# A hybrid decoder block on one core: the MLP's up projection with weights prepared four products ahead and its squares summed one per product, the down projection's buffers laid out anew

## The chip, the cores and the metric

The kernel runs on one core of a Trainium2 chip. The metric is the device time of one execution in microseconds (us). The engines named below are PE (TensorE, the matrix products; PEld is its loading of weights), DVE (VectorE), ACT (ScalarE), POOL (GpSimd) and SP (SyncE, which here issues nearly all transfers between HBM and the on-chip memory SBUF; SPq is its queue). Products are summed up in PSUM banks, which DVE and ACT read.

## The reference

One layer, on 2048 rows of 1024 columns, all float32. The part that the change touches is the last one:

```python
h = h + jnp.concatenate([y_s5, y_rwkv], axis=-1) @ w_out          # the output projection
hn = rms_norm(h, norm_ffn_g)
h = h + jnp.square(jax.nn.relu(hn @ w_up)) @ w_down               # 1024 -> 4096 -> 1024
return rms_norm(h, norm_final_g)
```

What comes ahead (a norm, an input projection, an S5 state-space mixer, an RWKV-7 mixer) is left as it is.

## The kernel before

**Products.** A float32 operand is split into a high half (`hi`, a cast to the type that PE takes, by ACT) and a low half (`lo = x - hi`, by DVE); a product of two operands is three products of halves, hi·hi, hi·lo and lo·hi. Above that the kernel multiplies 2x2 blocks by seven products in place of eight (Strassen's scheme in Winograd's form). The seven are numbered 1 to 7 and are written in the order `ORDER = (1, 5, 6, 2, 7, 3, 4)`; the sums of blocks that they need are made on POOL (`left_sums`, for the up weights: four sums in each set of seven) or on DVE or POOL (`right_sums`). Three PSUM tiles take the seven: `ps_ua` takes 1, then 6, 7 and 4 on top, and is read after each; `ps_ux` takes 5, then 3; `ps_ub` takes 2.

**Up projection, `mlp_up`.** Two halves of the rows (`hb`, 1024 rows each), and in each 16 steps of `f`: 32 blocks in all, here called block 0 to block 31. A block has seven products of 12 matmuls (128x128 by 128x512), 84 in all. The left operand is the weights: `ws()` loads them (`wraw`, seven buffers `raw`, which other loads share), makes the sums, and splits each into `wh` (ACT, L1423) and `wl` (DVE, L1424), in a ring of 16 buffers with the tag `ys`. `Ahead(ws(), UA)` runs that generator `UA` products ahead of the one that is written. The right operand is the normed activations `x1` to `x7`, split by `xs(hb)` once for each half of the rows: at the start, with the sums on DVE, and for the second half during block 15, with the sums on POOL. Blocks 1 and 2 also carry the last two pieces of the norm (`last_norm`: loads `hrow`, transposes `ps_tr`).

After product 2, 7, 3 and 4 one quarter of the block's result is complete: it gets relu and square (`finish`, ACT L1499 and L1500), as `q[1]`, `q[4]`, `q[3]` and `q[2]`. The down projection needs the sums of these quarters as its left operands: `operands` writes three of them plain to HBM (`hr_d`) and makes four sums, split into halves `hh` and `hl` in the same ring `ys` and written to HBM (`hs_d`). Before, three of the four sums come right after product 3, the fourth after product 4.

**Down projection, `mlp_down`.** Eight groups `gr` of the 4096 inner columns, and in each eight chunks `c` of 256 rows; a chunk has seven products of six matmuls. Weights `w_down` are loaded into `wraw` (two buffers of 1 MB), summed and split into `w0` to `w8`; the hidden operands are loaded back, the plain ones (`hr`) and split here, the summed ones (`hs`) as they are. The sums run in 16 tiles `acc` of 512 KB, which are loaded from `h_d` first. Product 1 of chunk 0 needs `w0` and the first `hr`.

**Order.** A scheduler orders the instructions of each engine; each engine then runs its own list strictly in that order, and waits on semaphores where one needs another's result. SP's list is one queue of issues. Pools of the down projection lie where pools of the up projection lay, and a tile can be filled only when the last use of the tiles under it is over. So the places of the pools in `mlp_down` decide how early its loads can be issued.

Of the kernel before, what the change touches and what calls it, by code (L numbers as in the profile page):

```python
# [7 lines left out]
F32 = mybir.dt.float32  # L8
# [3 lines left out]
ALU = mybir.AluOpType  # L12
# [3 lines left out]
P = 128  # L16
# [6 lines left out]
def pool_of(tc, **k):  # L23
    return tc.tile_pool(reuse_waits="tile", **k)
# [339 lines left out]
BT = 512  # L364
# [709 lines left out]
        yield  # L1074


UA, DW, DH = 2, 2, 3
WS, WA = 9, 3
OB = 256

# [241 lines left out]
def product(K, ps, left, right, start):  # L1322

    (lh, ll), (rh, rl) = left, right
    n = len(lh)
    for k in range(n):
        for i, (a, b) in enumerate(((lh, rh), (lh, rl), (ll, rh))):
            K.nc.tensor.matmul(ps, a[k], b[k], start=start and k + i == 0, stop=k == n - 1 and i == 2, skip_group_check=True)  # L1328
# [27 lines left out]
PLAIN = (1, 2, 4)  # L1356


def mlp_up(K, opened, h_dram, x2_dram, norm_g, w_up, hs_dram, hr_dram):


    nc, tc = K.nc, K.tc
    v, act, g = nc.vector, nc.scalar, nc.gpsimd
    H = KT // 2
    from contextlib import ExitStack
    with ExitStack() as st:
        pool_ = lambda **k: st.enter_context(pool_of(tc, **k))
        oc, oy, ops, last = opened
        xp, rp, cp, hp, psp = pool_(name="mux", bufs=1), pool_(name="mur", bufs=1), pool_(name="muc", bufs=1), pool_(name="muh", bufs=1), pool_(name="mups", bufs=2, space=PSUM)
# [57 lines left out]
        def last_norm(b):  # L1427

            ss, rows, junk = cp.tile([P, 2], F32, tag="ss", name="ss"), [raw([P, 1024], "hrow") for _ in range(2)], raw([P, 1024], "junk")
            for i, r in enumerate(rows):  # L1430
                nc.sync.dma_start(out=r, in_=h_dram[(2 * b + i) * P:(2 * b + i + 1) * P, :])
                act.activation(out=junk, in_=r, func=AF.Square, accum_out=ss[:, i:i + 1])
            rs = rms_rows(K, cp, ss, 2, 1024, "rstd")
            for i, r in enumerate(rows):
                v.tensor_scalar(out=r, in0=r, scalar1=rs[:, i:i + 1], scalar2=None, op0=ALU.mult)
            yield
            for k in range(KT):
                if k % 4 == 0:
                    o = raw([P, 4, 256], "xt")
                if k % 2 == 0:  # L1440
                    ps = ops.tile([P, BT], F32, tag="t2", bufs=1, name="ps_tr")
                    for i in range(4):
                        nc.tensor.transpose(out=ps[:, i * P:(i + 1) * P], in_=rows[i % 2][:, (k + i // 2) * P:(k + i // 2 + 1) * P], identity=K.ident)
                act.activation(out=o[:, k % 4], in_=ps[:, k % 2 * 256:k % 2 * 256 + 256], func=AF.Copy, scale=gain[:, k:k + 1])
                if k % 4 == 3:
                    nc.sync.dma_start(out=x2_dram[b // 2, :, k - 3:k + 1, b % 2 * 256:b % 2 * 256 + 256], in_=o)
                if k % 2:
                    yield
# [10 lines left out]
        def hid(name):  # L1459
            nonlocal ct  # L1460
            ct = (ct + 1) % 6
            return hp.tile([P, BT], F32, tag="o", bufs=3, name=name) if ct < 3 else oc[0].tile([P, BT], F32, tag=("g2h", "g2l", "g2s")[ct - 3], name=name)

        def operands(hb, fp, q, done):

            def plain(n):
                nc.sync.dma_start(out=hr_dram[hb, fp, PLAIN.index(n)], in_=q[n])

            def split_(n, o):
                hi, lo = (oy.tile([P, BT], F32R, tag="ys", bufs=16, name="h" + s) for s in "hl")  # L1470
                act.copy(out=hi, in_=o)  # L1471
                v.tensor_tensor(out=lo, in0=o, in1=hi.bitcast(F32), op=ALU.subtract)
                for i, t in enumerate((hi, lo)):
                    nc.sync.dma_start(out=hs_dram[hb, SPLIT.index(n), fp, i], in_=t.bitcast(F32))

            if done in (1, 4):
                plain(done)
            elif done == 3:
                a, c, d = q[1], q[3], q[4]
                s = hp.tile([P, BT], F32, tag="s", bufs=2, name="hs")  # L1480
                v.tensor_tensor(out=s, in0=c, in1=d, op=ALU.add)
                split_(5, s)
                v.tensor_tensor(out=c, in0=a, in1=c, op=ALU.subtract)
                split_(7, c)
                q["s2"] = s2 = hp.tile([P, BT], F32, tag="s", bufs=2, name="hs2")
                v.tensor_tensor(out=s2, in0=s, in1=a, op=ALU.subtract)
                split_(6, s2)
            else:
                plain(2)
                s = hp.tile([P, BT], F32, tag="s", bufs=2, name="hs3")  # L1490
                v.tensor_tensor(out=s, in0=q[2], in1=q["s2"], op=ALU.subtract)  # L1491
                split_(3, s)

        for hb in range(2):
            for f in range(0, 32, 2):
                q = {}

                def finish(o, name, src=None):
                    act.activation(out=o, in_=o if src is None else src, func=AF.Relu)  # L1499
                    act.activation(out=o, in_=o, func=AF.Square)  # L1500
                    q[name] = o
                    operands(hb, f // 2, q, name)

                def copy(ps, name):
                    o = hid(name)
                    act.copy(out=o, in_=ps)
                    return o

                A, X = (psp.tile([P, BT], F32, tag=n, bufs=2, name="ps_u" + n) for n in "ax")
                B = ops.tile([P, BT], F32, tag="o", bufs=2, name="ps_ub")  # L1510
                for n in ORDER:
                    lw = w.take()
                    if n not in x:
                        next(nx)
                    ps, start = {1: (A, True), 5: (X, True), 6: (A, False), 2: (B, True), 7: (A, False), 3: (X, False), 4: (A, False)}[n]
                    product(K, ps, lw, x[n], start)
                    if f in (2, 4) and hb == 0:
                        if n == 1:
                            ln = last_norm(NT // 256 - 3 + f // 2)
                        next(ln, None)  # L1520
                    if f == 30 and hb == 0:
                        if n == 1:
                            nx = xs(1)
                        next(nx)
                    if n == 1:
                        c1 = copy(A, "c1")
                    elif n == 5:
                        c5 = copy(X, "c5")
                    elif n == 6:
                        c2 = copy(A, "c2")  # L1530
                    elif n == 2:
                        v.tensor_tensor(out=c1, in0=c1, in1=B, op=ALU.add)  # L1532
                        finish(c1, 1)
                    elif n == 7:
                        v.tensor_tensor(out=c5, in0=c5, in1=A, op=ALU.add)
                        finish(c5, 4)
                    elif n == 3:
                        v.tensor_tensor(out=c2, in0=c2, in1=X, op=ALU.add)
                        finish(c2, 3)
                    else:  # L1540
                        finish(hid("c4"), 2, A)


def mlp_down(K, h_dram, hs_dram, hr_dram, w_down, fin_g, out):

    nc, tc = K.nc, K.tc
    v, act, g = nc.vector, nc.scalar, nc.gpsimd
    NG, NC = 8, NT // 256
    from contextlib import ExitStack
    with ExitStack() as st:  # L1550
        pool_ = lambda **k: st.enter_context(pool_of(tc, **k))

        hp, fp, wp1, rp, ap2 = (pool_(name="md" + n, bufs=1) for n in ("h", "f", "w1", "r", "a2"))
        wp2, wp3, ap1 = (pool_(name="md" + n, bufs=1, side="right") for n in ("w2", "w3", "a1"))
        psp = pool_(name="mdps", bufs=2, space=PSUM)
        wpool, apool = [wp1] * 6 + [wp2] + [wp3] * 2, [rp] * 2 + [ap1] * 8 + [ap2] * 2 + [wp3] * 4
        rows = lambda c: [(c // 4) * 1024 + i * BT + c % 4 * P for i in range(2)]

        def ws():
# [95 lines left out]
def hybrid_block(tc, a, cst, out):  # L1655
# [3 lines left out]
    with ExitStack() as st:  # L1659
# [44 lines left out]
        with ExitStack() as keep:  # L1704
            opened = out_proj(K, keep, a["x"], g_d, y_d, f_d, s_d, *A("g2", "ln_x_w", "ln_x_b", "w_glu", "b_glu", "s5_out_g", "w_out", "norm_ffn_g"), h_d, x2_d)
            mlp_up(K, opened, h_d, x2_d, a["norm_ffn_g"], a["w_up"], hs_d, hr_d)
        mlp_down(K, h_d, hs_d, hr_d, a["w_down"], a["norm_final_g"], out)


# [16 lines left out]
```

## Time and profile before

| | |
|---|---|
| median of 3 runs | 2716.64 us (2715.95 to 2719.07) |
| the profiled execution: its own time | 2711.46 us |
| its span, first to last instruction | 2709.7 us |
| mean granted PE clock | 0.965 of full speed |
| up projection, first matmul | 1266.5 us into the span |
| down projection, first matmul | 2029.1 us into the span |

A window row gives the length of a stretch, the busy time of each engine in it with the number of its instructions (x), the granted PE clock, the mean busy share of the 16 DMA engines and the GB/s that they moved. A group row gives an operation's count, its busy time and mean duration, and then the idle time of its engine just ahead of it with what ended it. A wait row gives who waited for whom: total, times, longest. A timeline row gives a start, a duration and the instruction.

### The profile page before, as it was taken

How to read it: one execution, taken by the hardware profiler on the slowest of the kernel's cores; microseconds unless marked ns; L12 is line 12 of the kernel's file. 1: busy time of each engine (PE TensorE's matmuls, PEld its weight loads, DVE VectorE, ACT ScalarE, POOL GpSimd, SP SyncE). 2: the span in 40 equal slices, each digit the busy share in tenths (PEclk: the TensorE clock that was granted, in tenths of full speed). 3: DMA queues.
4: the chain of work that ended last, by engine and by line, in shares of the span. 5: the costliest groups of instructions: out<-in, count | busy, mean ns of one | idle time of the engine just before them, and what ended most of it. 6: DMA issues, size and time to landing. Idle time of an engine off the chain costs nothing.

```text
span 2709.7 us, 38217 instructions
## 1 busy us (share of the span) xinstructions
PE 2486.5 (92%) x13084; PEld 2027.1 (75%) x13084; DVE 1910.2 (70%) x3177; ACT 1307.2 (48%) x2558; POOL 926.5 (34%) x812
## 2 busy tenths in 40 slices
PE   7999889998998989997899987999969999999997
PEld 7977667786998878886777765777747777777775
DVE  7478896688777777667677778776756666555665
ACT  5355545554544465553656555555543333332333
POOL 1068788502222233212322235322212323232333
PEclk9999989998999999999999998999989999999999
DMA  9556648996866464334655544555467555455545
GB/s 297 190 173 178 207 140 254 253 221 175 174 152 155 108 195 150 136 134 156 209 195 191 192 176 167 180 186 179 162 230 264 181 170 163 148 167 171 167 145 181
DMA packets 543187, 492.55 MB, mean 182 GB/s; under 512 B 187312, under 2 KB 445360, under 8 KB 542992
## 3 DMA queue, kind: packets, MB, share of 16 engines
q1 hardware_dynamic: 542704, 489.05, 58.0%
q8 instruction: 104, 1.70, 0.3%
q10 hardware_dynamic: 288, 1.05, 0.1%
q14 instruction: 91, 0.75, 0.1%
HBM read 304.27 MB, written 180.49 MB: 179 GB/s over the span
## 4 chain that ended last, share of the span: by engine, by line
PE 59%; DVE 16%; DMA 10%; issue 6%; ACT 5%; POOL 3%; SPq 1%; POOLq 0%; DVEq 0%; ACTq 0%
PE ps_ua L1328 12%; PE ps_da L1328 9%; PE ps_dx L1328 4%; PE ps_ux L1328 3%; PE ps_ub L1328 3%; PE ps_db L1328 2%; DMA wraw<-in_w_down 2%; PE ps_o L435 2%; PE ps_o L433 2%; PE ps_o L434 2%; DVE hs L1491 2%; PE ps_z L433 1%; PE ps_z L434 1%; PE ps_z L435 1%; PE ps_b L817 1%
## 5 line engine op out<-in xcount | busy, mean ns | idle before, releaser
L1605 POOL TENSOR_TENSOR acc<-acc,c 128x512 f32<-128x512 f32 x128 | 193.8, 1535 | 482.0 <-ACT c L1609 436.4
L1609 ACT COPY c<-ps_da 128x512 f32<-128x512 f32 x192 | 106.2, 588 | 266.0 <-PE ps_da L1328 265.5
L433 PE MATMUL ps_z<-xh,wh 128*128 128x512 f32 x448 | 184.9, 413 | 16.0 <-DVE zr L617 6.4
L435 PE MATMUL ps_z<-xh,wl 128*128 128x512 f32 x448 | 182.3, 407 | 0.0
L434 PE MATMUL ps_z<-xl,wh 128*128 128x512 f32 x448 | 181.4, 405 | 0.0
L1605 DVE TENSOR_TENSOR acc<-acc,ps_dx 128x512 f32<-128x512 f32 x128 | 87.6, 685 | 126.6 <-PE ps_dx L1328 121.4
L1424 DVE TENSOR_TENSOR wl<-wraw,wh 128x512 fp32r<-128x512 f32 x128 | 163.2, 1301 | 4.6 <-ACT wh L1423 1.8
L1300 POOL TENSOR_TENSOR ws<-wraw,ws 128x512 f32<-128x512 f32 x32 | 43.5, 1360 | 347.7 <-DVE wl L1424 342.1
L1499 ACT ACTIVATE c<-c 128x512 f32<-128x512 f32 x96 | 60.6, 631 | 165.8 <-DVE c L1532 101.5
L374 ACT CAST hh<-hr 128x512 fp32r<-128x512 f32 x96 | 59.6, 621 | 125.6 <-PE ps_da L1328 88.6
L433 PEld LDWEIGHTS ps_z<-xh,wh 128*128 128x128 f32 x448 | 87.7, 196 | 40.7 <-DVE zr L617 8.2
L609 DVE TENSOR_TENSOR wl<-wr,wh 128x1024 fp32r<-128x1024 f32 x56 | 85.2, 1522 | 36.4 <-ACT wh L608 34.3
L913 POOL TENSOR_TENSOR DT<-dtc,cst 128x128 f32<-128x128 f32 x128 | 56.0, 467 | 157.1 <-PE ps_pq L920 104.7
L433 PE MATMUL ps_o<-woh,ys 128*128 128x512 f32 x256 | 102.6, 401 | 1.5 <-ACT ys L1114 0.9
L434 PEld LDWEIGHTS ps_z<-xl,wh 128*128 128x128 f32 x448 | 87.7, 196 | 18.9 <-issue 0.9
L435 PEld LDWEIGHTS ps_z<-xh,wl 128*128 128x128 f32 x448 | 87.4, 195 | 19.2 <-issue 0.5
L434 PE MATMUL ps_o<-wol,ys 128*128 128x512 f32 x256 | 101.6, 398 | 0.0
L435 PE MATMUL ps_o<-woh,ys 128*128 128x512 f32 x256 | 100.7, 397 | 0.0
L1424 DVE TENSOR_TENSOR wl<-ws,wh 128x512 fp32r<-128x512 f32 x96 | 92.9, 968 | 1.7 <-ACT wh L1423 1.7
L1471 ACT CAST hh<-hs 128x512 fp32r<-128x512 f32 x96 | 59.8, 623 | 58.2 <-DVE hs L1491 49.7
L377 DVE TENSOR_TENSOR hl<-hr,hh 128x512 fp32r<-128x512 f32 x96 | 67.9, 712 | 26.1 <-ACT hh L374 25.9
L1500 ACT ACTIVATE c<-c 128x512 f32<-128x512 f32 x128 | 81.0, 633 | 3.5
(692 smaller groups left out, 8287.4 us busy)
## 6 DMA issues: line engine op xcount, KB each, us to landing
hs<-hs_d SPq DMA_DIRECT2D x128, 512.0 KB
wraw<-in_w_up SPq DMA_DIRECT2D x64, 512.0 KB
hs_d<-hh SPq DMA_DIRECT2D x128, 256.0 KB
hs_d<-hl SPq DMA_DIRECT2D x128, 256.0 KB
wr<-in_w_in SPq DMA_DIRECT2D x56, 512.0 KB
hr_d<-c SPq DMA_DIRECT2D x96, 256.0 KB
hr<-hr_d SPq DMA_DIRECT2D x96, 256.0 KB
xrow<-in_x SPq DMA_DIRECT2D x32, 512.0 KB
```

Of the source, the lines that this page charges most:

```text
L377: (lo_eng or nc.vector).tensor_tensor(out=lo, in0=raw, in1=hi.bitcast(F32), op=ALU.subtract)
L433: K.nc.tensor.matmul(out, lh, rh, start=i == 0, stop=False)
L434: K.nc.tensor.matmul(out, lh, rl, start=False, stop=False)
L435: K.nc.tensor.matmul(out, ll, rh, start=False, stop=i == n - 1)
L609: v.tensor_tensor(out=wl, in0=wr, in1=wh.bitcast(F32), op=ALU.subtract)
L1328: K.nc.tensor.matmul(ps, a[k], b[k], start=start and k + i == 0, stop=k == n - 1 and i == 2, skip_group_check=True)
L1424: v.tensor_tensor(out=lo, in0=o, in1=hi.bitcast(F32), op=ALU.subtract)
L1471: act.copy(out=hi, in_=o)
L1499: act.activation(out=o, in_=o if src is None else src, func=AF.Relu)
L1500: act.activation(out=o, in_=o, func=AF.Square)
L1605: add = lambda eng, o, s: eng.tensor_tensor(out=o, in0=o, in1=s, op=ALU.add)
L1609: act.copy(out=t, in_=ps)
```

## The change

Three edits. `UA` goes from 2 to 4. `operands` becomes a generator that makes one of the four sums at each step; it is advanced after product 4 of its own block and after products 1, 5 and 6 of the next (`pend`), and the plain quarters are written right where they are finished. The pools of `mlp_down` get other places: the pool of `wraw` and the first two `acc` tiles (`rp`) moves down on the left side, below the weights' pool, and the `acc` tiles and the later weights change sides.

```diff
-UA, DW, DH = 2, 2, 3
+UA, DW, DH = 4, 2, 3
@@ mlp_up
-        def operands(hb, fp, q, done):
-
-            def plain(n):
-                nc.sync.dma_start(out=hr_dram[hb, fp, PLAIN.index(n)], in_=q[n])
+        def operands(hb, fp, q):
...
-            if done in (1, 4):
-                plain(done)
-            elif done == 3:
-                a, c, d = q[1], q[3], q[4]
-                s = hp.tile([P, BT], F32, tag="s", bufs=2, name="hs")
-                v.tensor_tensor(out=s, in0=c, in1=d, op=ALU.add)
-                split_(5, s)
-                v.tensor_tensor(out=c, in0=a, in1=c, op=ALU.subtract)
-                split_(7, c)
-                q["s2"] = s2 = hp.tile([P, BT], F32, tag="s", bufs=2, name="hs2")
-                v.tensor_tensor(out=s2, in0=s, in1=a, op=ALU.subtract)
-                split_(6, s2)
-            else:
-                plain(2)
-                s = hp.tile([P, BT], F32, tag="s", bufs=2, name="hs3")
-                v.tensor_tensor(out=s, in0=q[2], in1=q["s2"], op=ALU.subtract)
-                split_(3, s)
-
+            a, c, d = q[1], q[3], q[4]
+            s = hp.tile([P, BT], F32, tag="s", bufs=2, name="hs")
+            v.tensor_tensor(out=s, in0=c, in1=d, op=ALU.add)
+            split_(5, s)
+            yield
+            v.tensor_tensor(out=c, in0=a, in1=c, op=ALU.subtract)
+            split_(7, c)
+            yield
+            v.tensor_tensor(out=s, in0=s, in1=a, op=ALU.subtract)
+            split_(6, s)
+            yield
+            s3 = hp.tile([P, BT], F32, tag="s", bufs=2, name="hs3")
+            v.tensor_tensor(out=s3, in0=q[2], in1=s, op=ALU.subtract)
+            split_(3, s3)
+
+        pend = iter(())
...
-                    operands(hb, f // 2, q, name)
+                    if name in PLAIN:
+                        nc.sync.dma_start(out=hr_dram[hb, f // 2, PLAIN.index(name)], in_=o)
...
                         finish(hid("c4"), 2, A)
+                        pend = operands(hb, f // 2, q)
+                    if n in (4, 1, 5, 6):
+                        next(pend, None)
+        for _ in pend:
+            pass
@@ mlp_down
-        hp, fp, wp1, rp, ap2 = (pool_(name="md" + n, bufs=1) for n in ("h", "f", "w1", "r", "a2"))
-        wp2, wp3, ap1 = (pool_(name="md" + n, bufs=1, side="right") for n in ("w2", "w3", "a1"))
+        hp, fp, rp, wp1, ap2 = (pool_(name="md" + n, bufs=1) for n in ("h", "f", "r", "w1", "a2"))
+        ap1, wp2 = (pool_(name="md" + n, bufs=1, side="right") for n in ("a1", "w2"))
...
-        wpool, apool = [wp1] * 6 + [wp2] + [wp3] * 2, [rp] * 2 + [ap1] * 8 + [ap2] * 2 + [wp3] * 4
+        wpool, apool = [wp1] * 4 + [wp2] * 5, [rp] * 2 + [ap1] * 10 + [ap2] * 4
```

The lists of the engines are the same up to the start of the up projection, and PE's is the same again after the down projection's first chunks. Three places show what moves in between. The changed kernel's line numbers differ by a few: L1535 becomes L1531, L1481 L1475, L1472 L1469, L1491 L1485.

DVE in a block of the steady part, before: from `c += ps_ua` (product 7 complete) on, the four sums of the squares with their low halves, and only then the weights.

```order
L1535 TENSOR_TENSOR c_17623<-c_17623,ps_ua 128x512
L1481 TENSOR_TENSOR hs<-c_17642,c_17623 128x512
L1483 TENSOR_TENSOR c_17642<-c_17605,c_17642 128x512
L1486 TENSOR_TENSOR hs_17724<-hs,c_17605 128x512
L1472 TENSOR_TENSOR hl<-hs,hh 128x512
L1472 TENSOR_TENSOR hl<-c_17642,hh 128x512
L1472 TENSOR_TENSOR hl<-hs_17724,hh 128x512
L1424 TENSOR_TENSOR wl<-ws,wh 128x512
L1491 TENSOR_TENSOR hs_17754<-c_17750,hs_17724 128x512
L1472 TENSOR_TENSOR hl<-hs_17754,hh 128x512
L1424 TENSOR_TENSOR wl<-ws,wh 128x512
L1424 TENSOR_TENSOR wl<-wraw,wh 128x512 x2
```

The same place now:

```order
L1531 TENSOR_TENSOR c_17599<-c_17599,ps_ua 128x512
L1475 TENSOR_TENSOR hs<-c_17624,c_17599 128x512
L1478 TENSOR_TENSOR c_17624<-c_17572,c_17624 128x512
L1469 TENSOR_TENSOR hl<-hs,hh 128x512
L1424 TENSOR_TENSOR wl<-wraw,wh 128x512
L1481 TENSOR_TENSOR hs<-hs,c_17572 128x512
L1469 TENSOR_TENSOR hl<-c_17624,hh 128x512
L1424 TENSOR_TENSOR wl<-ws,wh 128x512
L1469 TENSOR_TENSOR hl<-hs,hh 128x512
L1424 TENSOR_TENSOR wl<-wraw,wh 128x512
L1528 TENSOR_TENSOR c_17749<-c_17749,ps_ub 128x512
L1485 TENSOR_TENSOR hs_17803<-c_17717,hs 128x512
```

The weights' low halves now stand between the sums, one after each. Counted through the lists: where `c += ps_ua` stands, the `wl` ahead of it reach two products past the matmuls that it waits for before, and some four to seven now; at `c += ps_ub` they reach four before, two to six now. Where the second half's activations are split, the reach falls to 0.2 in block 15 and 0.4 in block 16 now, and is two to four before.

SP where the up projection ends, before. `c_19690` is the last quarter of block 31, finished after the last matmul of the up projection; `hr` and `hs` are the down projection's first operands, `wraw` its first weights.

```order
L1467 DMA hr_d<-c_19690 128x512
L1474 DMA hs_d<-hh 128x512
L1474 DMA hs_d<-hl 128x512
L1580 DMA hs<-hs_d 128x4x256 x2
L1584 DMA hr<-hr_d 128x2x256 x2
L1580 DMA hs<-hs_d 128x4x256
L1584 DMA hr<-hr_d 128x2x256
L1565 DMA wraw<-in_w_down 128x2x1024 x2
L1601 DMA acc_19772<-h_d 128x1024
```

The same place now; `c_19636` is the last quarter here, `c_19515` and `c_19542` those after products 2 and 7 of block 31.

```order
L1566 DMA wraw<-in_w_down 128x2x1024 x2
L1471 DMA hs_d<-hh 128x512
L1471 DMA hs_d<-hl 128x512
L1602 DMA acc_19737<-h_d 128x1024
L1602 DMA acc_19739<-h_d 128x1024
L1636 DMA fin<-in_norm_final_g 128x1024
L1498 DMA hr_d<-c_19515 128x512
L1498 DMA hr_d<-c_19542 128x512
L1498 DMA hr_d<-c_19636 128x512
L1471 DMA hs_d<-hh 128x512
L1471 DMA hs_d<-hl 128x512
L1471 DMA hs_d<-hh 128x512
```

The weights' loads have moved from behind the last quarter and seven loads of operands to a place ahead of block 31's first finished quarter; the first load of `hr` is the row after these, behind the last quarter, while before it stood ahead of that one.

DVE at the same boundary now, from the third weight's low half to the first down operand's low half (`hl<-hr`). Before, `hl<-hr` stood ahead of all of the down weights' work.

```order
L377 TENSOR_TENSOR w1l<-wraw,w1h 128x1024
L1475 TENSOR_TENSOR hs<-c_19567,c_19542 128x512
L1311 TENSOR_TENSOR wraw<-wraw 128x2x512
L1478 TENSOR_TENSOR c_19567<-c_19515,c_19567 128x512
L1469 TENSOR_TENSOR hl<-hs,hh 128x512
L377 TENSOR_TENSOR w2l<-wraw,w2h 128x1024
L1481 TENSOR_TENSOR hs<-hs,c_19515 128x512
L1469 TENSOR_TENSOR hl<-c_19567,hh 128x512
L1318 TENSOR_TENSOR wraw<-wraw 128x2x512
L1485 TENSOR_TENSOR hs_19662<-c_19636,hs 128x512
L1469 TENSOR_TENSOR hl<-hs,hh 128x512
L377 TENSOR_TENSOR hl<-hr,hh 128x512
```

Ahead of these stand `c += ps_ua` of block 31, two more sums of weights and the low half of `w3`.

## The prediction

> **What bounds the kernel now.** I read the page's first part and the chain that ended last, then windows cut at the up projection's blocks, then the waits in each.
>
> ```profile
> PE 2486.5 (92%) x13084; PEld 2027.1 (75%) x13084; DVE 1910.2 (70%) x3177; ACT 1307.2 (48%) x2558; POOL 926.5 (34%) x812
> PE 59%; DVE 16%; DMA 10%; issue 6%; ACT 5%; POOL 3%; SPq 1%; POOLq 0%; DVEq 0%; ACTq 0%
> ```
>
> PE is busy 92% of the span and leads the chain, so time can come only from its gaps. The windows: blocks 0 to 2; 3 to 14; 15 and 16; 17 to 30; 31; from the up projection's last matmul to the down projection's first; the start of the down projection.
>
> ```profile
> 1266.50:1355.60 89.10, 67.86 (x273) 52.12 (x272) 66.62 (x64) 48.08 (x87) 37.14 (x20) 0.87 0.57 192
> 1355.60:1611.40 255.80, 243.82 (x1009) 185.75 (x1009) 184.79 (x217) 151.50 (x266) 74.02 (x48) 1.00 0.54 189
> 1611.40:1682.10 70.70, 47.37 (x169) 35.73 (x168) 63.21 (x50) 38.36 (x58) 37.02 (x16) 0.81 0.46 156
> 1682.10:1980.40 298.30, 284.89 (x1178) 216.54 (x1177) 215.81 (x252) 175.46 (x308) 85.50 (x56) 1.00 0.50 177
> 1980.40:2005.60 25.20, 23.50 (x97) 17.44 (x95) 14.31 (x21) 13.90 (x25) 1.29 (x1) 1.00 0.41 147
> 2005.60:2029.10 23.50, 0.00 (x0) 0.00 (x0) 6.20 (x10) 6.25 (x10) 0.00 (x0) 0.55 1.00 354
> 2029.10:2068.00 38.90, 37.56 (x144) 28.67 (x144) 30.93 (x32) 13.55 (x20) 7.34 (x5) 0.92 1.00 380
> ```
>
> Columns: length; busy PE, PEld, DVE, ACT, POOL with counts; PE clock; DMA share; GB/s. Blocks 3 to 14 and 17 to 30 take 255.8/12 and 298.3/14, both 21.31 us a block. The chain gives the pace of matmuls that wait for nothing:
>
> ```profile
> 1374.70 8.35 PE ps_ua L1328 x36
> ```
>
> 8.35/36 is 0.232, so a block's 84 matmuls could take 19.48: a steady block loses 1.83. The waits of blocks 17 to 30 (total, times, longest) name the cause:
>
> ```profile
> PEld ps_ua L1328 <- ACT wh L1423: 13.9, 14, 1.0
> PEld ps_ux L1328 <- DVE wl L1424: 11.1, 14, 0.9
> PE ps_ua L1328 <- ACT wh L1423: 7.8, 14, 0.6
> PEld ps_ux L1328 <- ACT wh L1423: 5.1, 14, 0.4
> ```
>
> Fourteen times in fourteen blocks, halves of weights. The timeline of one block shows why they are late:
>
> ```profile
> 1754.73 0.62 ACT L1471 CAST hh<-hs 128x512 fp32r<-128x512 f32 x1 [1.70 <-DVE hs L1491]
> 1755.26 0.61 ACT L1423 CAST wh<-ws 128x512 fp32r<-128x512 f32 x1
> 1755.93 0.50 PE L1328 MATMUL ps_ua<-x6h,wh 128*128 128x512 f32 x1 [0.56 <-ACT wh L1423]
> ```
>
> ACT stood 1.70 us for the last sum of the squares, with the weights' cast queued behind it, and PE waited for that cast.
>
> **The change part by part.**
>
> *Weights four ahead, sums one per product: the steady blocks.* Nothing is added in arithmetic: per block the same seven `wh`, seven `wl`, four sums with four `hh` and four `hl`, four POOL sums and eleven stores. Only places change. The lists show the weights prepared four to seven products (of 12 x 0.232 = 2.8 us) past PE where `c += ps_ua` stands, and never under two in a steady block. Two is 5.6 us, while a steady block's longest waits are 1.0. So the weights' waits should go, and PE's own pace be what is left: 19.48, plus the waits for a PSUM tile's copies that no prefetch removes. I take 19.8, nearest to the pace row; bounds 19.48 and 20.8 (0.5 saved, if most of it turns into other waits). 26 blocks x (21.31 - 19.8) = 39, bounds 13 and 48. Block 31 took 25.2 for 96 matmuls (its own and product 4 of block 30), at the pace 22.3; half of the 2.9 should go: 1.5. What covers this is room on DVE and ACT: 215.81/14 = 15.4 and 175.46/14 = 12.5 us a block, 78% and 63% of 19.8. Late next is DVE.
>
> Moved past each other on SP are these stores and the weights' loads, which wait for a `raw` buffer; a store behind such a load leaves late, and then its buffer in the ring of 16 comes free late, on which the `wl` eight pairs later waits. Eight pairs are 8/11 of a block, 14 us; I cost it at nothing.
>
> *The same, blocks 0 to 2.* 89.1 us against 58.4 at the pace. The waits there:
>
> ```profile
> PE ps_ua L1328 <- DVE wl L1424: 6.5, 1, 6.5
> PE ps_ux L1328 <- ACT wh L1423: 6.4, 2, 5.0
> PE ps_ua L1328 <- ACT wh L1423: 3.3, 1, 3.3
> PE ps_tr L1443 <- DVE hrow L1435: 3.1, 2, 2.8
> ```
>
> The first three (nearly all in block 0) stay: the lists of DVE and ACT are the same until seven weights are made. The 1.4 left of the second and the 3.1 for the transposes (of block 2, now written one block later on PE) should go, with the slow pace behind them: 7, bounds 0 and 11.
>
> *The same, blocks 15 and 16.* 70.7 against 39; DVE is busy 63.21 of it, so DVE is the bound there, because POOL's sums run beside it:
>
> ```profile
> PE ps_ux L1328 <- ACT wh L1423: 9.2, 2, 4.6
> PE ps_ua L1328 <- DVE c L1535: 7.6, 1, 7.6
> L1403 DVE TENSOR_TENSOR x6l<-xraw,x6h 128x1024 fp32r<-128x1024 f32 x2 | 4.5, 2268 | 0.0
> L1403 DVE TENSOR_TENSOR x5l<-xraw,x5h 128x1024 fp32r<-128x1024 f32 x2 | 2.4, 1219 | 0.6 <-ACT x5h L1402 0.6
> ```
>
> The work stays (fourteen such halves, 1.2 to 2.3 us); four more products of weights made beforehand take some 4 us off DVE. The lists leave the weights 0.2 to 0.4 of a product ahead here, so waits remain. DVE's 63.2 less that is the floor, 59: I take 7, bounds -5 (a new wait of the longest kind in these rows) and 12. A gap here costs twice, since PE restarts slowly:
>
> ```profile
> 1650.30 0.79 PE L1328 MATMUL ps_ua<-x4h,wh 128*128 128x512 f32 x1 [7.56 <-DVE c L1535]
> 1650.89 0.63 PE L1328 MATMUL ps_ua<-x4l,wh 128*128 128x512 f32 x1
> 1651.32 0.63 PE L1328 MATMUL ps_ua<-x4h,wl 128*128 128x512 f32 x1
> ```
>
> The pace is 0.43 instead of 0.232 behind it.
>
> *Buffers of the down projection.* The boundary, before:
>
> ```profile
> 2005.15 0.39 PE L1328 MATMUL ps_ua<-x4h,wl 128*128 128x512 f32 x1
> 2005.61 0.39 SPq L1584 DMA_DIRECT2D hr<-hr_d  x1
> 2008.73 0.62 ACT L374 CAST hh<-hr 128x512 fp32r<-128x512 f32 x1
> 2019.09 1.30 SPq L1565 DMA_DIRECT2D wraw<-in_w_down  x2
> PE ps_da L1328 <- ACT w0h L374: 23.6, 1, 23.6
> ```
>
> The operand `hr` was there at 2008.7, the weights' load was issued at 2019.1, and PE waited 23.6. Now that load is issued when block 31's product 5 is over, some 14 us before the end, so `w0` is ready in time. Late next is `hr`: it stands behind the last quarter's store and the sum for 5, and DVE has about eleven operations ahead of its `hl` (seven of 1.1, the rest of 0.6), so the first down matmul should start 10 us behind the last up matmul: 13 less. But the window rows show the DMA engines 1.00 busy from 2005.6 to 2068, and twelve `acc` loads stand ahead of chunk 2's operands. What leaves that stretch is only what is now loaded earlier, 2 MB of weights and 1 MB of `acc`: 3.1 MB at 380 GB/s is 8. I take the smaller, 8; bounds 2 and 14.
>
> *Sum.* 39 + 1.5 + 7 + 7 + 8 = 62.5. The profiled execution took 2711.5, so 2649; it lies 5.2 below the median of the runs, 2716.6, against which the forecast is **2654**. All bounds together: 2716.6 - 86 = 2630 and 2716.6 - 11 = 2706.
>
> **A rule against it.** DVE's steady rows show what POOL does to it, count, mean ns:
>
> ```profile
> L1424 DVE TENSOR_TENSOR wl<-wraw,wh 128x512 fp32r<-128x512 f32 x56 | 70.9, 1292 | 2.5 <-ACT wh L1423 1.1
> L1472 DVE TENSOR_TENSOR hl<-hs,hh 128x512 fp32r<-128x512 f32 x42 | 28.9, 687 | 9.6 <-ACT hh L1471 9.6
> L1535 DVE TENSOR_TENSOR c<-c,ps_ua 128x512 f32<-128x512 f32 x14 | 9.6, 688 | 28.4 <-PE ps_ua L1328 28.4
> L1481 DVE TENSOR_TENSOR hs<-c,c 128x512 f32<-128x512 f32 x14 | 9.7, 693 | 19.1 <-ACT c L1500 19.1
> ```
>
> The same shape takes 0.69 where POOL rests and 1.29 where it works beside it. The Trainium skill (SBUF — State Buffer, "Who interferes with whom") says that a DVE instruction with two SBUF inputs contends with a GpSimd one that reads SBUF, and that whichever issues second is blocked for the whole of the first. By that rule the loss could reach POOL's whole time in each block, and prefetching cannot shrink it; the trace agrees in kind (1.29 against 0.69), not in full.
>
> **The rivals.**
>
> A: POOL holds DVE for all of its time. DVE per block: 18 operations x 0.69 = 12.4, plus POOL's 85.5/14 = 6.1, is 18.5, plus the 28.4/14 = 2.0 that it stands for `ps_ua`: 20.5. The steady term becomes 26 x 0.8 = 21: 2654 + 18 = 2672. For it: the 1.29. Against: DVE is measured at 15.4, with POOL's four sums in it. This is the result that the rule above would give.
>
> B: the lead does not arrive, because the ring of 16 is shared: five pairs of weights ahead, one in use and the squares' pairs leave none, and the lists do show `wl` waiting for PE. Then the steady term is 0 and blocks 15 and 16 gain 0: 2654 + 47.5, about 2700.
>
> C, slower: DVE becomes the bound by standing in its list. With `wl` between the sums, POOL's work falls on these too; if the four sums take 1.5 in place of 0.69, DVE has 15.4 + 3.2 = 18.6, and with today's 5.9 idle (21.31 - 15.4) a block takes 24.5: 26 x 3.2 = 83 lost, 15 gained elsewhere, some 2780. It decides from the point where work and standing pass 21.31, 0 above today's. Against: 3.4 of the 5.9 are waits for `ps_ua` and its relu (28.4 + 19.1 over 14), which come earlier when PE does.
>
> D: the pools' new places bring nothing, as chunk 2 waits for the 8: 2662, inside the range.
>
> **How the numbers follow.** Forecast (with D) 0.62; A 0.18; B 0.07; C 0.05; better than all my bounds 0.03; about the same by mishap 0.05. The likeliest is 2654. Its own spread, and A, reach from 2626 (PE's bare pace and a short boundary) to 2690; that leaves B, C and the rest out. 0.2% is 5.4 us, about what a measurement can tell. Faster by more: the first three and the fifth, 0.90; within: 0.04; slower: 0.06.
>
> **What would show it.** Right: steady blocks of 19.5 to 20.1 us; `wh` and `wl` gone from PE's waits there; blocks 15 and 16 at 58 to 66; the first down matmul 8 to 12 us behind the last up one, and a new wait of PE for `hr` or `hs` in the first three chunks. Wrong: steady blocks above 20.5 with PE waiting for `c` or `wl` (A, C); `wl` waiting on PE (B); DVE rows of the sums at over 1 us (C); a boundary above 18.

## The result, and the profile after

The changed kernel takes 2643.60 us (median of 4 runs, 2635.71 to 2647.79) against 2717.86 of before in the same set (4 runs, 2715.95 to 2721.99). The ratio is 0.9721, with a 95% interval from 0.9696 to 0.9747. The forecast was 2654, with a range from 2626 to 2690. The profiled execution took 2643.06, its span is 2641.3: 68.4 us shorter than the profiled span of before.

The first part of its page:

```profile
PE 2459.0 (93%) x13084; PEld 2032.2 (77%) x13084; DVE 1845.4 (70%) x3177; ACT 1301.6 (49%) x2558; POOL 917.0 (35%) x812
```

Its windows, cut at counts of matmuls (252 for blocks 0 to 2, then 1260, 1428, 2604 and the last one of the up projection; the down projection's first matmul, its 127th; and 126 further on):

```profile
1272.40:1351.70 79.30, 64.64 (x270) 51.04 (x269) 65.47 (x69) 48.57 (x86) 37.51 (x21) 0.89 0.54 182
1351.70:1588.40 236.70, 235.77 (x1025) 190.26 (x1024) 158.51 (x216) 151.41 (x272) 74.16 (x50) 1.00 0.64 216
1588.40:1648.00 59.60, 44.72 (x169) 33.26 (x168) 57.97 (x48) 35.75 (x57) 33.66 (x15) 0.89 0.54 177
1648.00:1922.00 274.00, 273.07 (x1178) 220.23 (x1177) 187.24 (x255) 172.81 (x309) 83.70 (x56) 1.00 0.57 194
1922.00:1942.90 20.90, 19.41 (x84) 15.45 (x83) 12.98 (x18) 13.48 (x22) 0.00 (x0) 1.00 0.73 264
1942.90:1953.10 10.20, 0.43 (x2) 0.00 (x1) 10.09 (x13) 5.51 (x10) 0.00 (x0) 0.76 0.82 297
1953.10:1994.60 41.50, 32.49 (x126) 25.20 (x126) 21.79 (x28) 13.43 (x20) 6.95 (x5) 0.87 1.04 388
1994.60:2026.10 31.50, 31.46 (x127) 25.27 (x128) 13.75 (x20) 7.50 (x13) 6.95 (x6) 0.92 0.57 185
```

Two rows stand out. In the steady windows (the second and the fourth of these) PE is busy 235.77 of 236.70 and 273.07 of 274.00. The seventh, the down projection's first 126 matmuls, has DMA at 1.04 and PE busy only 32.49 of 41.50.

All waits of PE in blocks 17 to 30:

```profile
PE ps_ua L1328 <- ACT c L1502: 0.9, 1, 0.9
```

DVE's two groups of weights there:

```profile
L1424 DVE TENSOR_TENSOR wl<-wraw,wh 128x512 fp32r<-128x512 f32 x57 | 51.0, 895 | 7.4 <-ACT wh L1423 3.5 <-DMA hs_d<-hh 1.7 <-PE ps_ux L1328 1.2
L1424 DVE TENSOR_TENSOR wl<-ws,wh 128x512 fp32r<-128x512 f32 x42 | 38.6, 921 | 4.4 <-ACT wh L1423 4.0 <-ACT c L1494 0.3
```

The four rows of `wh` and `wl` are gone; blocks 3 to 14 have the same single row of 0.9. The `wl` made from `wraw`, which took 1292 ns, takes 895, nearer to the 0.69 us of the operations away from POOL; the other group stays as it was (918 before). One of the four sums, `hs` at L1491, took 1510 ns before and takes 694 at L1485 now.

The same places in both profiled executions, by the times of matmuls of the same count:

| stretch | before, us | after, us | difference | forecast |
|---|---|---|---|---|
| blocks 0 to 2 | 91.9 | 79.3 | -12.6 | -7 |
| blocks 3 to 14 | 255.8 | 236.8 | -19.0 | -18 |
| blocks 15 and 16 | 70.7 | 59.6 | -11.1 | -7 |
| blocks 17 to 30 | 298.3 | 273.9 | -24.3 | -21 |
| block 31 | 22.0 | 21.0 | -1.0 | -1.5 |
| last up matmul to first down matmul | 24.0 | 10.2 | -13.8 | -13 |
| first 168 down matmuls (four chunks' worth) | 45.1 | 53.5 | +8.4 | +5 |

(The prediction gives the two steady rows as one, 39, and the last two as one, 8.) Unrounded, that adds up to 73.53. The up projection begins 5.85 later in the profile of after, and the rest is 0.74 shorter: 73.53 - 5.85 + 0.74 = 68.4. Ahead of the up projection the instruction lists are the same; its first matmul came between 1266.5 and 1273.5 us in all the profiles of this study, and at 1272.5 and 1267.5 in two kernels that differ in the down projection alone, so those 5.85 are taken for scatter and no effect of the change.

What took the place of the wait for `w0`, in PE's waits from the last up matmul to 2026 us:

```profile
PE ps_da L1328 <- ACT hh L374: 18.5, 2, 9.8
```

The same on the timelines, rows of ACT, SP and PE:

```profile
1952.45 0.62 ACT L374 CAST hh<-hr 128x512 fp32r<-128x512 f32 x1 [1.74 <-DMA hr<-hr_d]
...
1965.76 9.31 SPq L1602 DMA_DIRECT2D acc<-h_d  x8
1976.03 0.38 SPq L1566 DMA_DIRECT2D wraw<-in_w_down  x1
1977.26 1.60 SPq L1602 DMA_DIRECT2D acc<-h_d  x2
1981.15 3.16 SPq L1585 DMA_DIRECT2D hr<-hr_d  x3
1993.21 2.13 ACT L374 CAST hh<-hr 128x512 fp32r<-128x512 f32 x3 [1.17 <-DMA hr<-hr_d]
1994.64 0.79 PE L1328 MATMUL ps_da<-w0h,hh 128*128 128x512 f32 x1 [8.73 <-ACT hh L374]
```

The first `hr` holds the first down matmul. Behind 126 matmuls PE's list has the first product of chunk 4 and then the last three products of chunk 2. The operands of all of these are issued from 1981.15 on, behind ten `acc` loads and two weights' loads; the `hr` land some 12 us later, and PE stands 8.73. (The expectations call this the gap ahead of chunk 2.)

### The profile page after: what moved, and what is told of

Same layout as the page of the kernel before. It is cut to its first block, busy times and chain, and to the rows that moved or that the text cites. A ratio compares the mean times of both kernels' runs of the same rounds, so it can differ in the third digit from the quotient of the medians.

```text
span 2641.3 us, 38268 instructions
## 1 busy us (share of the span) xinstructions
PE 2459.0 (93%) x13084; PEld 2032.2 (77%) x13084; DVE 1845.4 (70%) x3177; ACT 1301.6 (49%) x2558; POOL 917.0 (35%) x812
## 3 DMA queue, kind: packets, MB, share of 16 engines
q10 hardware_dynamic: 288, 1.05, 0.1%
## 5 line engine op out<-in xcount | busy, mean ns | idle before, releaser
L1424 DVE TENSOR_TENSOR wl<-wraw,wh 128x512 fp32r<-128x512 f32 x128 | 124.3, 972 | 13.3 <-ACT wh L1423 8.7
L1294 POOL TENSOR_TENSOR ws<-ws,wraw 128x512 f32<-128x512 f32 x32 | 53.4, 1667 | 210.0 <-DVE wl L1424 209.8
L374 ACT CAST hh<-hr 128x512 fp32r<-128x512 f32 x96 | 59.6, 621 | 126.5 <-PE ps_da L1328 91.4
L1494 ACT ACTIVATE c<-c 128x512 f32<-128x512 f32 x96 | 60.5, 632 | 107.1 <-DVE c L1531 56.9
L913 POOL TENSOR_TENSOR DT<-dtc,cst 128x128 f32<-128x128 f32 x128 | 55.8, 466 | 159.1 <-PE ps_pq L920 105.5
L1469 DVE TENSOR_TENSOR hl<-hs,hh 128x512 fp32r<-128x512 f32 x96 | 74.4, 775 | 23.4 <-ACT hh L1468 21.4
L1424 DVE TENSOR_TENSOR wl<-ws,wh 128x512 fp32r<-128x512 f32 x96 | 83.9, 880 | 8.6 <-ACT wh L1423 7.4
```

Source lines behind the costliest of these rows:

```text
L374: nc.scalar.copy(out=hi, in_=raw)
```

## The experiments

**One part of the change alone.** The four runs below share one set: before 2716.25 us (13 runs). For each the table shows the time, and by matmul counts the same stretches in us; the last row is repeated from above, with its own set.

| | time, us | ratio to before (95%) | blocks 0-2 | a steady block, 3-14 / 17-30 | blocks 15, 16 | last up to first down | first 168 down |
|---|---|---|---|---|---|---|---|
| before | 2716.25 | | 91.9 | 21.31 / 21.31 | 70.7 | 24.0 | 45.1 |
| UA = 4 only | 2643.48 | 0.9742 (0.9706 to 0.9779) | 79.9 | 19.72 / 19.61 | 62.7 | 25.4 | 43.3 |
| squares only | 2656.51 | 0.9779 (0.9754 to 0.9804) | 80.1 | 19.90 / 19.69 | 63.4 | 16.2 | 53.3 |
| buffers only | 2710.14 | 0.9984 (0.9971 to 0.9998) | 92.9 | 21.44 / 21.30 | 71.9 | 6.6 | 55.8 |
| UA and squares | 2644.02 | 0.9737 (0.9712 to 0.9762) | 80.5 | 19.73 / 19.57 | 60.0 | 23.3 | 42.7 |
| whole change | 2643.60 | 0.9721 (0.9696 to 0.9747) | 79.3 | 19.73 / 19.57 | 59.6 | 10.2 | 53.5 |

*UA = 4 only:*

```diff
-UA, DW, DH = 2, 2, 3
+UA, DW, DH = 4, 2, 3
```

> Only UA = 4; sums of the squares and buffers as before. Theory (the weights' lead alone removes their waits): wh and wl gone from PE's waits in the steady blocks, 19.6 to 20.1 us a block instead of 21.3; blocks 0 to 2 and 15, 16 keep most of their gain (8 to 20 together of the 23.7 that the whole change gave); the boundary stays at 24 us. About 2655, from 2648 to 2672. Rival (the sums standing together in DVE's and ACT's lists are the cause, and a longer lead only stands in the same queue): 20.8 us a block or more, over 2690.

The two theories' dividing line, 2672 against 2690, is clear: 2643.5. It is 12 better than the 2655 expected: blocks 0 to 2 keep 12.0 of their 12.6 and blocks 15 and 16 8.0 of 11.1, the upper end of the 8 to 20 expected of them together, and the steady blocks lie near the lower end of their range. PE's waits of blocks 17 to 30:

```profile
PE ps_ux L1328 <- ACT wh L1423: 0.8, 1, 0.8
PE ps_ua L1328 <- ACT wh L1423: 0.4, 1, 0.4
```

The window:

```profile
1647.10:1921.60 274.50, 273.28 (x1178) 220.04 (x1177) 176.85 (x254) 176.08 (x312) 75.73 (x57) 1.00 0.55 192
```

As far as these runs can tell, one line of the change gives as much as the whole.

*Squares only* (the generator `operands` with its `yield`s, UA = 2, buffers as before):

> Only the sums of the squares, one per product; UA = 2 and buffers as before. Theory (lead): the weights come as late as before, though ACT no longer stands 1.7 us for the last sum with a cast behind it, so half of the steady loss may go: 20.4 to 21.3 us a block, 2690 to 2717. Rival (the order of the sums does the work): 19.6 to 20.0 a block, wh and wl gone from PE's waits, below 2672.

Here my theory was wrong and the rival right for the steady part: 19.90 and 19.69 a block, and the waits of blocks 17 to 30 are down to one row:

```profile
PE ps_ub L1328 <- DVE wl L1424: 1.5, 5, 0.5
```

Its start of the down projection (16.2 and 53.3) differs though the buffers lie as before, since the lists there moved too; the sum, 69.5, is before's 69.1. In time it stays 13 behind the version with UA = 4 alone, by the medians. The two profiled executions lie 5 apart, 3.4 of it in the steady blocks; the profiled one was the fastest of its four, so where the rest lies isn't seen.

So either edit removes nearly all of the same waits; they don't add up. Why is seen when, for each product, the end of its `wh` cast is taken from the start of its first matmul with it: the time that the weight lay ready. Medians over blocks 17 to 30, in us, in the order in which the weights are made:

| product | 1 | 5 | 6 | 2 | 7 | 3 | 4 |
|---|---|---|---|---|---|---|---|
| before | 8.3 | 0.1 | 0.1 | 0.1 | 7.0 | 3.8 | 11.6 |
| UA = 4 only | 5.5 | 5.4 | 12.3 | 2.8 | 4.4 | 1.4 | 10.5 |
| squares only | 4.3 | 8.9 | 4.7 | 3.2 | 8.8 | 2.6 | 10.6 |
| whole change | 4.7 | 8.0 | 14.5 | 11.3 | 11.6 | 7.6 | 16.8 |

Before, the weights of three products arrive as they are wanted, all of them queued behind the sums of the squares; the other four lie ready for 3.8 us or more. What was short was mainly a few operations' place. Either way of spreading them leaves 1.4 us or more in the median; the whole change leaves 4.7 or more, and PE gains little from the difference. In all three versions the scheduler also moved PE's own products (in block 20, for one, product 4 falls behind product 5 of the next block). No run here keeps PE's list and moves only the weights, so how much of the readiness comes from that stays open.

There is a second possible cause, which the prediction did not look for here. The last sum of the squares, for which ACT stood 1.70 us, ran beside one of POOL's sums:

```profile
1752.86 1.29 POOL L1300 TENSOR_TENSOR ws<-wraw,ws 128x512 f32<-128x512 f32 x1 [11.62 <-DVE wl L1424]
1753.07 1.63 DVE L1491 TENSOR_TENSOR hs<-c,hs 128x512 f32<-128x512 f32 x1 [0.35 <-ACT c L1500]
L1491 DVE TENSOR_TENSOR hs<-c,hs 128x512 f32<-128x512 f32 x14 | 21.1, 1510 | 6.7 <-ACT c L1500 6.7
```

With UA = 4 alone it takes 0.69, with the squares alone 0.68. So up to 0.8 of the 1.83 us that a steady block lost may come from this overlap with POOL, which both edits happened to end. No run moves that sum of POOL alone, so the two causes are not told apart.

*Buffers only* (the three lines of `mlp_down`):

> Only the new places of the down projection's buffers. Theory (the boundary's gain is given back by transfers that are not shorter): last up matmul to first down matmul 10 to 14 us instead of 24, then a gap of 7 to 10 us ahead of chunk 2; net 3 to 8 faster, 2709 to 2715; up blocks 0 to 30 unchanged within 3 us. Rival (without the lead of four, block 31 pays for the down weights' casts and sums that now run in it): block 31 2 to 6 us longer, net nothing, 2714 to 2722.

2710.1, 6 faster, as the theory had it, with the way there sharper than expected: PE starts 6.6 behind the last up matmul, 17.4 earlier, and 10.7 of it are given back in the first 168 matmuls, where PE waits for `hh` and a weight (waits, and then their window):

```profile
PE ps_da L1328 <- ACT hh L374: 10.9, 2, 6.2
PE ps_dx L1328 <- ACT w5h L374: 2.2, 1, 2.2
```

```profile
2017.20:2073.00 55.80, 47.32 (x169) 36.58 (x170) 28.69 (x38) 15.48 (x24) 8.96 (x7) 0.84 0.96 350
```

Block 31 took 22.2 against 22.0: the rival's 2 to 6 us of casts in it were not seen.

*The whole change but the buffers:*

> The whole change but the new places of the buffers. Theory (boundary worth 5 net): 2649, from 2645 to 2653; boundary 24 us, no gap of 9 us ahead of chunk 2. Rival (the boundary is worth the 13.8 that lie between the two matmuls, and the gap ahead of chunk 2 would be there anyhow): 2657 or more. Second rival (worth nothing): 2641 to 2645.

2644.0, where the second rival said 2641 to 2645 and mine 2645 to 2653: on top of the other two edits, the buffers' new places bring nothing that these runs can tell from zero (0.9737 and 0.9721, with overlapping intervals). PE waits 22.9 for `w0h` and then runs through (waits, then the windows of the wait and of the first 168 matmuls):

```profile
PE ps_da L1328 <- ACT w0h L374: 22.9, 1, 22.9
```

```profile
1938.60:1961.90 23.30, 0.42 (x3) 0.01 (x1) 6.86 (x12) 6.33 (x11) 0.00 (x0) 0.57 0.98 347
1961.90:2004.60 42.70, 41.67 (x168) 32.61 (x169) 35.10 (x37) 16.06 (x23) 11.37 (x7) 0.95 0.97 365
```

While PE waits, DMA is at 0.98 and brings the `acc` tiles. The time is the same whether PE stands for 23 us once, or for 10 and 9.

**What the rest of the time hangs on.** The next four share a set: before 2718.18 (7 runs).

*The changed kernel again:*

> The changed kernel once more, beside the three runs below on the same chip. Both theories: 2638 to 2648; first down matmul 10 us behind the last up one, a gap of 9 us ahead of chunk 2.

2643.96 (2634.64 to 2647.29), ratio 0.9721 (0.9699 to 0.9742).

*POOL's sums twice*, in `left_sums`, for three of the four:

```diff
     s = new()
-    eng.tensor_tensor(out=s, in0=c, in1=d, op=ALU.add)
+    for _ in range(2):
+        eng.tensor_tensor(out=s, in0=c, in1=d, op=ALU.add)
```

> The changed kernel, with three of the four sums that POOL makes for each block of weights made twice, so POOL has some 10 us of work a block instead of 6. Theory (a weight is ready 2.5 us or more ahead of its matmul, mostly 5 to 15, so slower DVE operations beside POOL cost PE nothing): wl at 1.0 to 1.3 us instead of 0.9, but steady blocks 19.5 to 20.0 us; the time within 8 us of the changed kernel's, the rest of it in blocks 0, 15 and 16. Rival A of the prediction (POOL holds DVE for all of its time): DVE has 18.5 + 4.4 = 22.9 a block and becomes the bound, 26 x 3 = 78 us slower, about 2720.

2654.8, 11 slower, of which 3.6 us lie in blocks 0 to 2 and 2.8 in block 17; the 8 expected were exceeded. But the steady blocks are 19.63 and 19.89 us:

```profile
1356.90:1592.50 235.60, 235.60 (x1026) 190.39 (x1025) 188.82 (x218) 152.30 (x276) 132.83 (x87) 1.00 0.64 217
1653.50:1931.90 278.40, 274.09 (x1177) 219.94 (x1176) 213.11 (x256) 174.61 (x312) 155.01 (x101) 1.00 0.55 191
```

POOL is busy 155.0 in blocks 17 to 30 instead of 83.7, DVE 213.1 instead of 187.2: DVE pays 25.9 for 71.3 us of POOL, 0.36 of it; in blocks 3 to 14 30.3 for 58.7, 0.52. Rival A needs all of it, 22.9 us a block and 78 us in sum. The Trainium skill (SBUF — State Buffer, "Who interferes with whom") calls the ports that the two engines share an exclusive lock, and says that whoever issues first has them for the whole instruction while the other is blocked; here DVE's part of that is a third to a half of POOL's time, and what POOL's own operations lost was not measured.

*The second half's activation sums on DVE:*

```diff
-            parts = [right_sums((v, g)[hb], q) for q in qs]
+            parts = [right_sums(v, q) for q in qs]
```

> The changed kernel, with the eight sums for the second half's activations (blocks 15 and 16) on DVE instead of POOL. Theory (DVE is the bound there, 58.0 of 59.6 us, and part of that is slowness beside POOL: 1.2 us an activation's half alone, 1.8 to 2.3 beside it): DVE pays 8 x 1.2 = 10 and gets back 14 x 0.6 = 8, so blocks 15 and 16 take 57 to 64, the time within 5 us. Rival (work of DVE alone counts, and its rows' length is waiting that would be there anyhow): 67 to 72 in blocks 15 and 16, 8 to 12 us slower.

2631.85 (2628.94 to 2634.16), ratio 0.9681 (0.9667 to 0.9695): 12 faster than the changed kernel, and better than both theories had it. Blocks 15 and 16 take 49.6 us instead of 59.6. Their window:

```profile
1588.70:1638.30 49.60, 43.05 (x170) 32.90 (x169) 47.63 (x55) 34.84 (x54) 20.87 (x6) 0.93 0.64 212
```

DVE's groups for the halves of one activation and of the squares in these blocks, in the changed kernel:

```profile
L1403 DVE TENSOR_TENSOR x7l<-xraw,x7h 128x1024 fp32r<-128x1024 f32 x2 | 4.7, 2326 | 0.0
L1469 DVE TENSOR_TENSOR hl<-hs,hh 128x512 fp32r<-128x512 f32 x6 | 9.6, 1602 | 0.0
```

The same here, and one of the groups of sums that DVE took over:

```profile
L1403 DVE TENSOR_TENSOR x7l<-xraw,x7h 128x1024 fp32r<-128x1024 f32 x2 | 2.4, 1221 | 0.0
L1469 DVE TENSOR_TENSOR hl<-hs,hh 128x512 fp32r<-128x512 f32 x6 | 4.2, 694 | 0.0
L1309 DVE TENSOR_TENSOR xraw<-xraw 128x1024 f32<-128x1024 f32 x2 | 2.5, 1228 | 0.0
```

DVE makes the eight sums as well (55 operations in the window, 48 in the changed kernel) and is busy 10.3 us less, 47.63 against 57.97. I had counted only the activations' halves as slowed; `hl` fell from 1602 to 694 ns as well. One of these sums costs DVE 1.23 us, while on POOL it took 2.8 to 3.1:

```profile
L1315 POOL TENSOR_TENSOR xraw<-xraw 128x1024 f32<-128x1024 f32 x2 | 6.2, 3092 | 0.0
```

(This row is that of the second run of the changed kernel, in blocks 15 and 16.)

*The `acc` loads behind the operands:*

```diff
-                  with tc.issue_after(first.ins) if c else ExitStack():
+                  with tc.issue_after((last_hs[0, c // 2 * 2 - 2] if c >= 4 else first).ins) if c else ExitStack():
```

(`last_hs[gr, c]` is the load of the last `hs` of a chunk.)

> The changed kernel, with the loads of the acc tiles of chunks 4 to 7 of the first group queued behind the operands of the chunks two to three ahead of them, in place of ahead of chunk 2's operands. Theory (the gap ahead of chunk 2 is 4 MB of acc in the way, and not the bytes in all): gap ahead of chunk 2 below 3 us, first 168 down matmuls 44 to 48 us instead of 53.5, the time 5 to 9 below the changed kernel's in the same set: about 2636. Rival (the transfers of the stretch end as late in any order): the gap goes to another chunk, and the time stays within 3 us.

2632.60 (2631.44 to 2638.57), ratio 0.9689 (0.9673 to 0.9704), 11 faster than the changed kernel: a little more than the 5 to 9 expected. The first 168 down matmuls take 44.6 us, as before the change. SP's queue and PE's first wait behind it, on the timeline:

```profile
1958.93 5.98 SPq L1604 DMA_DIRECT2D acc<-h_d  x6
1965.39 1.87 SPq L1566 DMA_DIRECT2D wraw<-in_w_down  x2
1968.16 3.10 SPq L1587 DMA_DIRECT2D hr<-hr_d  x3
...
1976.87 3.64 SPq L1604 DMA_DIRECT2D acc<-h_d  x4
1984.41 0.51 PE L1328 MATMUL ps_da<-w0h,hh 128*128 128x512 f32 x1 [1.86 <-ACT hh L374]
```

The window of the first 126 matmuls:

```profile
1949.60:1984.40 34.80, 31.76 (x126) 24.30 (x126) 19.97 (x24) 12.89 (x20) 6.42 (x5) 0.95 1.05 381
```

The DMA engines are as full as in the changed kernel (1.05), and the kernel loads the same bytes in all; the order decided. With the loads, the scheduler also put the first of the three `hh` ahead of a weight's cast (`w8h`) on ACT. That is not what let PE go on: its 1.86 here are for the second `hh`, which still stands behind `w8h`, and `w8h` waited 1.97 for a sum of DVE.

**Both together, and the old places.** One set, before 2715.82 (9 runs).

> The changed kernel with both edits that helped: the second half's activation sums on DVE, and the acc loads of chunks 4 to 7 behind operands. Theory (the one lies in blocks 15 and 16, the other in the first chunks of the down projection, and they share no resource): the two gains add up, 12.1 + 11.4 below the changed kernel's 2644, so about 2620, from 2615 to 2626. Rival (the time won at the one place is waited out at the other, since the transfers of the down projection start earlier but not more than the up projection's stores let them): 2628 to 2632, no better than the best of the two.

2621.33 (2618.01 to 2627.35), ratio 0.9649 (0.9629 to 0.9668): the gains add up, blocks 15 and 16 at 49.6 and the first 168 down matmuls at 44.0. It is the fastest version here, 22 under the changed kernel.

*The `acc` loads behind the operands, with the old places of the buffers:*

> The lead of four and the sums one per product, with the buffers of the down projection where they were before, and the acc loads of chunks 4 to 7 behind operands. Theory (in the old places PE's wait of 23 us for w0 covers the acc loads, so their order is worth nothing there; the new places are worth 11 once the acc loads stand behind): within 4 of the version with the old places alone, 2640 to 2648. Rival (the order of the acc loads is worth its 11 by itself, and the new places are worth nothing): about 2633.

2644.66 (2639.43 to 2645.37), ratio 0.9732 (0.9713 to 0.9751). Nothing is won, since PE stands 22.9 for `w0h` again, as in the version with the old places alone.

Beside the other two edits, the new places and the order of the loads are each worth nothing that these runs can tell from zero, and 11 together.

## Why the prediction was right, and where not

The direction, the mechanism and the size were right: 2643.6 lies 10 under the 2654 and well inside the range. The misses mostly do not cancel: by the two profiles the steady blocks, blocks 0 to 2 and blocks 15 and 16 gave 4.3, 5.6 and 4.1 more than their terms, block 31 and the boundary 0.5 and 2.6 less. Point by point:

- *Steady blocks*, 39 forecast, 43.3 measured. The waits named are gone, and nothing came in their place but one of 0.9. The 19.8 was too careful: 19.73 and 19.57 came, 0.25 and 0.09 above the pace of 19.48. What the step had wrong is the attribution: it priced the lead and the sums' spreading as one cause, and either does nearly all of it alone; and it did not see POOL's possible part in the 1.70 us that ACT stood for the last sum (the sum took 1.51 us before, 0.69 now).
- *Blocks 0 to 2*, 7 forecast, 12.6 measured, over its bound of 11. The term mis-sized is block 2: its 84 matmuls went from 29.3 to 20.0 us. I had counted the two waits for `hrow`, 3.1, and some slow pace behind them; 9.3 went, three times that row. That block 0 keeps its waits was right (6.2, 5.2 and 3.2 us still stand there).
- *Blocks 15 and 16*, 7 forecast, 11.1 measured. The floor that the prediction named, DVE's work of about 59, was reached (57.97 busy of 59.6). I had kept nearly 5 back for waits that the lists let me expect; they came, but beside work that DVE had to do anyhow. That the floor itself was made of waiting for POOL, and fell by 10 when the sums moved to DVE, I had not seen.
- *Boundary*, 8 forecast as 13 less, cut for chunk 2; 13.8 less 8.4, 5.4, measured by the two profiles, and none against the version with the old places. The first down matmul came 10.2 behind the last up one (10 forecast) and the wait was for `hr`, as forecast; "twelve acc loads stand ahead of chunk 2's operands" named the second gap, though PE stood there at a product of chunk 4 that its list has ahead of chunk 2's last three. The mis-sized part is the cut, 5 for 8.4: I counted bytes, where the order of the loads decides; with the order mended, the first 168 matmuls give nothing back (44.6).
- *Rival A* fell by the doubled sums (19.63 and 19.89 us a block in place of 22.9). *B* fell by the readiness: 4.7 us or more, the ring is no limit. *C* fell by DVE's rows: the sums at L1475, L1478, L1481 and L1485 take 0.69 to 0.72, and the one of them that had taken 1.51 before got shorter. *D* gave 2662 and so missed the time, but its statement on the buffers, that the first chunks take back what the start gains, is what the runs show.

Two more things explain block 2. The prediction left out one row of the waits of before:

```profile
PE ps_tr L1443 <- ACT xt L1444: 1.9, 2, 0.9
```

It belongs to block 2, where PE stood 5.0 us in all. And part of the gain only moved: block 2 had 16 of the norm's transposes before and has 4 now, while block 3, which had none, has 16 and takes 21.27 us, where blocks 4 and 5 take 19.48. Those 1.8 us make up 0.15 of the 0.25 by which blocks 3 to 14 lie above the pace.

## What to carry to other kernels

Where PE waits for an operand, take for every product the time for which the operand lay ready. If a few stand at 0.1 us and the rest at several, look at their place in the lists first: here either of two edits that spread them brought nearly the whole gain of the steady blocks, and the second added little. Look also at what runs beside the operation that they are queued behind. And a load that is issued earlier helps only as far as the loads behind it still come in the order in which they are needed: here two edits worth nothing each were worth 11 us together.

## What the runs showed of the hardware that I had not expected

Giving the slower engine some of DVE's work cost DVE more than it spared. With eight 128x1024 sums on POOL, some of DVE's operations beside them lasted 1.6 and 2.3 us instead of 0.69 and 1.22; with the sums on DVE it was busy 10.3 us less in the same two blocks. In the other blocks, doubling three of POOL's four smaller sums cost 0.36 to 0.52 us of DVE for each us of POOL, and where DVE had room, in blocks 3 to 14, that cost no time (19.63 us a block against 19.73).
